# The first two products of a decoder layer: input in column quarters, both products fed together, zero products ahead of the input

## The chip, the cores and the metric

The kernel runs on one core of one Trainium2 chip. The metric is the device time of one execution in microseconds; a lower time is better. The time before is the median of three runs.

## The reference, cut to what matters

One inference step of a hybrid decoder layer, for a prompt of 512 tokens and 8 sample tokens (520 columns in all), width 1024. The normalised input is multiplied by one wide matrix, whose column groups feed three branches; the branches are gated, merged and added to the input, and a convolutional feed-forward network follows.

```python
h = rmsnorm(x, p['norm1_g'])
z = h @ p['w_in']                      # za, zq, zk, zv, zc, zg
za, zq, zk, zv, zc, zg = jnp.split(z, SPLITS, axis=-1)
...
lam = (jnp.exp(jnp.sum(p['b_lq1'].astype(f32) * p['b_lk1'].astype(f32)))
       - jnp.exp(jnp.sum(p['b_lq2'].astype(f32) * p['b_lk2'].astype(f32))) + lam_init)
o = diff_attention(q, k_all.reshape(b, -1, N_HEADS_B, 2, HEAD_DIM_B), v_all, start_pos, lam)
...
x = x + merged @ p['w_o']
f, conv_tail = conv_ffn(rmsnorm(x, p['norm2_g']), conv_prefix, p['f_up'], p['f_conv_w'], p['f_conv_b'], p['f_down'])
```

## The kernel before

All work is laid out with features on the 128 partitions and the 520 tokens as columns. The program is a list of slots (`plan`), each of which is one product: 128 columns of a weight matrix (eight blocks of 128 rows, 512 KB) by the whole activation. `zq0` to `zq3`, `zk0` to `zk3`, `zv0` to `zv3`, `z0` to `z3` and so on are slots 0, 1, 2, ... of the input projection, one for each 128 output columns.

Products keep float32 accuracy by splitting both operands into a high and a low part. A weight block `raw` becomes `wh` (a cast on ScalarE, L95) and `wl` (the difference, L96). An activation row block k becomes `Hh[k]` (`hi`, ScalarE, L450: the transposed input `xT` times the norm's gain) and `Hl[k]` (`lo`, VectorE, L453). A block (k, t) of a product is a pair of matmuls of 260 columns (L187): t = 0 is `wh` by high, t = 1 `wh` by low, t = 2 `wl` by high. So a slot is 24 pairs, 48 matmuls, in one of two PSUM accumulators (`pg`, two buffers); `evac` empties it.

`run_slot(n)` emits, in this order: the split of the weights of slot n+1, the load of those of slot n+3 (three `raw` buffers), the slot's `before` functions, then the 24 pairs with steps of the waiting chains in between. A chain is a generator: `advance` resumes the first ones of the turn after each k. A plain `yield` ends a chain's part in this slot; `yield True` puts it at the end of the turn of the same slot (`wait(4)` yields True four times). Each engine executes what was emitted for it in that order.

`begin` is written out by hand: it loads x, transposes it on TensorE into `xT` through four PSUM banks (`TP`, tag "t", handed out in rotation), and does the first product, `g_first`, interleaved with that. Its inputs come as two column halves for each 128-token tile, each followed by half of the first weights. GpSimd makes `wl` of the first product and, for k = 7, `h7` and the low part. Then it calls slot 0's `before` functions (`consts2`: constants built on GpSimd and VectorE; `chan_rows`), starts `norm1` (sums of squares on ScalarE, `ss` cleared on VectorE first) and evacuates the first product on ScalarE. `norm1` keeps reading the untransposed x.

`lam_rows` starts in slot 1: it issues five small loads, and after one yield computes lambda on VectorE and ScalarE (L332 to L338) and spreads it over the partitions by a matmul, `t_lam` (L341). `dec_softmax` (L818) transposes the scores `S_all` of cached keys into three banks (`s_dec`, `t_nk`); `pool` (L924) does a 128x512 product `s_c` (L946) for each of four groups; `attn` takes two banks for scores (`s_a`), later one for transposes (`t_a`) and one for outputs (`o_a`).

Of the kernel before, what the change touches and what calls it, by code (L numbers as in the profile page):

```python
# [45 lines left out]
class Layer:  # L46
# [276 lines left out]
    def lam_rows(self):  # L323
        nc, i = self.nc, self.i
        q = nc.sync
        self.ptab = self.C("ptab", [1, NB * NPG], I32)
        q.dma_start(self.ptab, i["page_table"].rearrange("(o a) b -> o (a b)", o=1))
        lr = self.T("lr", n=256)[0:1].rearrange("p (a d) -> p a d", a=4)
        for n, nm in enumerate(("b_lq1", "b_lq2", "b_lk1", "b_lk2")):
            q.dma_start(lr[:, n, :], i[nm])  # L330
        yield
        nc.vector.tensor_scalar(out=self.ptab, in0=self.ptab, scalar1=0, scalar2=N_POOL - 1, op0=ALU.max, op1=ALU.min)  # L332
        ls = self.C("ls", [1, 4])
        nc.vector.tensor_tensor(out=lr[:, 0:2], in0=lr[:, 0:2], in1=lr[:, 2:4], op=ALU.mult)
# [83 lines left out]

    def begin(self):
        nc, i = self.nc, self.i  # L420
        flat = lambda t: t.rearrange("p a b -> p (a b)")
        xr = [flat(self.B(f"x{t}"))[:, 0:D] for t in range(NT)] + [flat(self.B("xs"))[0:NB, 0:D]]
        nr = self.T("n1r", n=P)[0:KD]
        nc.scalar.dma_start(nr, i["norm1_g"][0].rearrange("(k p) -> k p", p=P))
        nc.scalar.dma_start(xr[NT], i["x_sample"].rearrange("b o d -> (b o) d"))
        for a in range(2):
            c = slice(a * 512, (a + 1) * 512)
            for t in range(NT):
                nc.sync.dma_start(xr[t][:, c], i["x_prompt"][0, t * P:(t + 1) * P, c])
            self.w_load(0, a)  # L430
        self.w_load(1)
        self.w_load(2)
        self.consts()
        n1 = self.C("n1", [P, KD])
        xT = [self.B("xT0"), self.B("xT1")]
        H = self.hp.tile([P, KD, NTOK], F32R, tag="Hh", name="Hh"), self.hp.tile([P, KD, NTOK], F32R, tag="Hl", name="Hl")
        self.hx = [(H[0][:, k], H[1][:, k]) for k in range(KD)]

        def turn(t, a, act):
            n = P if t < NT else NB  # L440
            tp = self.TP(f"t_x{t}{a}")
            for k in range(4):
                c = (4 * a + k) * P
                nc.tensor.transpose(tp[:, k * n:(k + 1) * n], xr[t][:, c:c + P], self.ident[0:n, 0:n])
            (nc.scalar.copy if act else nc.vector.tensor_copy)(
                xT[a][:, :, t * P:t * P + n], tp[:, 0:4 * n].rearrange("p (k t) -> p k t", k=4)
            )
# [7 lines left out]
        raw = self.raw.pop(0)  # L455
        wh, wl = (self.ws.tile([P, KD, P], F32R, tag=f"w{x}", name=f"w{x}_first") for x in "hl")
        wsp = lambda c: self.split(wh[:, c:c + 4], wl[:, c:c + 4], raw[:, c:c + 4], pool=True)
        ps = self.G("g_first")
        mm = lambda k, t: self.mm(ps, wh, wl, self.hx, k, t, k == t == 0, k == KD - 1 and t == 1)
        for t in range(NT):  # L460
            turn(t, 0, t == 1)
            if t == 1:
                tp = self.TP("t_n1")
                nc.tensor.transpose(tp[:, 0:KD], nr, self.ident[0:KD, 0:KD])
                nc.vector.tensor_copy(n1, tp[:, 0:KD])
                turn(NT, 0, 0)
        wsp(0)
        hi(0)
        turn(0, 1, 0)
        mm(0, 0)  # L470
        lo(0)
        hi(1)
        turn(1, 1, 0)
        turn(NT, 1, 0)
        hi(2)
        turn(2, 1, 0)
        mm(1, 0)
        turn(3, 1, 0)
        mm(2, 0)
        hi(3)  # L480
        mm(3, 0)
        wsp(4)
        for k in range(4, KD):
            hi(k)
        h7 = self.T("h7", n=NTOK)
        nc.gpsimd.tensor_scalar(out=h7, in0=xT[1][:, 3], scalar1=n1[:, 7:8], scalar2=None, op0=ALU.mult)
        nc.gpsimd.tensor_tensor(out=H[1][:, 7], in0=h7, in1=H[0][:, 7], op=ALU.subtract)
        for k in range(1, 7):
            lo(k)
        self.w_split(1)  # L490
        self.w_load(3)
        for k in range(4):
            mm(k, 2)
        for k in range(4):
            mm(k, 1), mm(k + 4, 0)
        for t in (2, 1):
            for k in range(4, KD):
                mm(k, t)
        self.slots[0][5]()
        self.start(self.norm1(xr, xT))  # L500
        self.slots[0][4](ps[:, :, 0:HALF])

    def norm1(self, xr, xT):
        nc = self.nc
# [313 lines left out]
    def dec_softmax(self, b0, b1):  # L818
        nc = self.nc
        n = 8 * (b1 - b0)  # L820
        m = n // 2
        if b0 == 0:
            self.wdz = self.B("wdz").rearrange("p a b -> p (a b)")
            nc.gpsimd.memset(self.wdz, 0.0)
            self.wn = self.C("wn", [NB, NH])
        pt = self.K(f"dp{b0}").rearrange("p a b -> p (a b)")[0:n]
        sp = [self.TP(f"s_dec{a}") for a in range(2)]
        for g in range(NPG):
# [21 lines left out]
        for g in range(NPG):  # L850
# [11 lines left out]
            out=wn, in_=wp[0:NB, 256:256 + m].rearrange("p (b h) -> p h b", h=NH), op=ALU.add, axis=AX.X  # L862
# [61 lines left out]
    def pool(self, j, win, zp, zs):  # L924
        nc = self.nc
# [3 lines left out]
        for l in range(j + 1):  # L929
            sh, lo = 1 << l, (2 << l) - 1  # L930
# [21 lines left out]
        ps = self.TP("s_cs")  # L952
        for g in range(4):
# [3 lines left out]
            out=ocs, in0=ps[:, 0:32].rearrange("p (j b) -> p j b", j=4),  # L957
            in1=self.cols[:, 8:12].unsqueeze(2).to_broadcast([P, 4, NB]), op=ALU.mult,
# [393 lines left out]
    def run(self):  # L1352
        self.plan()
        with self.tc.manual_schedule():
            self.begin()
            for n in range(1, len(self.slots)):
                self.cur = self.slots[n][0]
                self.run_slot(n)
            while self.chains:
                self.turn = list(self.chains)  # L1360
                self.advance()
                while self.micro:
                    self.small(1)
# [34 lines left out]
```

## Time and profile before

| | |
|---|---|
| median of 3 runs | 903.24 us (902.83 to 903.92) |
| the profiled execution | 902.99 us, of which the span from first to last instruction 901.0 us |
| TensorE busy in the span | 881.0 us (98%) |
| VectorE, ScalarE, GpSimd busy | 578.0, 340.1, 25.3 us |
| mean granted TensorE clock | 0.993 of full speed |
| 0 to 100 us: TensorE, VectorE, ScalarE busy | 90.94, 61.12, 47.24 us |
| 200 to 300 us: TensorE, VectorE, ScalarE busy | 97.18, 90.69, 49.35 us |

Times in the views count from the span's start. A busy TensorE is not TensorE at its peak: matmuls overlap, and at half clock one takes about twice as long. The idle time in front of an instruction is put down to what released it.

### The profile page before, as it was taken

How to read it: one execution, taken by the hardware profiler on the slowest of the kernel's cores; microseconds unless marked ns; L12 is line 12 of the kernel's file. 1: busy time of each engine (PE TensorE's matmuls, PEld its weight loads, DVE VectorE, ACT ScalarE, POOL GpSimd, SP SyncE). 2: the span in 40 equal slices, each digit the busy share in tenths (PEclk: the TensorE clock that was granted, in tenths of full speed). 3: DMA queues.
4: the chain of work that ended last, by engine and by line, in shares of the span. 5: the costliest groups of instructions: out<-in, count | busy, mean ns of one | idle time of the engine just before them, and what ended most of it. 6: DMA issues, size and time to landing. Idle time of an engine off the chain costs nothing.

```text
span 901.0 us, 17445 instructions
## 1 busy us (share of the span) xinstructions
PE 881.0 (98%) x7151; PEld 843.7 (94%) x7151; DVE 578.0 (64%) x970; ACT 340.1 (38%) x537; POOL 25.3 (3%) x80
## 2 busy tenths in 40 slices
PE   7899999999999999999999999999999999999998
PEld 6899987898998989889989999999999999999998
DVE  5367899879899533425775577775347777774332
ACT  4455433437532412212334334443124444442122
POOL 4000000000000000000000000000000000000000
PEclk9899999999999999999999999999999999999999
DMA  6636663426675566753443323323333333333242
GB/s 189 219 111 201 202 199 96 152 86 204 216 232 158 165 194 215 237 162 93 147 130 94 94 82 106 88 84 91 91 95 94 95 94 95 94 92 91 80 113 60
DMA packets 170467, 120.31 MB, mean 134 GB/s; under 512 B 6232, under 2 KB 149909, under 8 KB 169860
## 3 DMA queue, kind: packets, MB, share of 16 engines
q1 hardware_dynamic: 170157, 118.47, 43.5%
q8 instruction: 56, 0.92, 0.4%
q10 hardware_dynamic: 231, 0.73, 0.3%
q14 instruction: 23, 0.19, 0.1%
HBM read 112.45 MB, written 7.14 MB: 133 GB/s over the span
## 4 chain that ended last, share of the span: by engine, by line
PE 86%; DVE 9%; ACT 2%; issue 1%; DMA 1%; SPq 0%; ACTq 0%; DVEq 0%
PE g_f L187 28%; PE g_d L187 13%; PE g_ag L187 5%; PE g_bg L187 5%; PE g_o L187 5%; PE g_cg L187 3%; PE g_ap L187 3%; PE g_zk L187 3%; PE g_u L187 3%; PE g_va L187 3%; PE g_z L187 2%; PE g_zq L187 2%; PE o_dec L786 2%; PE g_zv L187 1%; DVE S_all L745 1%
## 5 line engine op out<-in xcount | busy, mean ns | idle before, releaser
L187 PE MATMUL g_f<-H2h,wl_f 128*128 128x260 f32 x704 | 141.9, 283 | 0.0
L187 PE MATMUL g_f<-H2h,wh_f 128*128 128x260 f32 x704 | 141.8, 282 | 0.0
L187 PE MATMUL g_f<-H2l,wh_f 128*128 128x260 f32 x704 | 141.7, 283 | 0.0
L187 PEld LDWEIGHTS g_f<-H2h,wh_f 128*128 128x128 f32 x704 | 108.5, 188 | 0.0
L187 PEld LDWEIGHTS g_f<-H2h,wl_f 128*128 128x128 f32 x704 | 108.5, 188 | 0.0
L187 PEld LDWEIGHTS g_f<-H2l,wh_f 128*128 128x128 f32 x704 | 108.2, 188 | 0.0
L187 PE MATMUL g_d<-ah,wh_d 128*128 128x260 f32 x340 | 69.2, 285 | 0.0
L187 PE MATMUL g_d<-al,wh_d 128*128 128x260 f32 x340 | 68.4, 283 | 0.0
L187 PE MATMUL g_d<-ah,wl_d 128*128 128x260 f32 x340 | 68.3, 282 | 0.0
L92 DVE SCALAR_TENSOR_TENSOR cv<-up,cv,cv 128x511 f32<-128x511 f32 x88 | 65.6, 746 | 2.9 <-ACT cv L1157 1.3
L95 ACT CAST wh_f<-wr_f 128x1024 fp32r<-128x1024 f32 x44 | 46.1, 1048 | 52.7 <-PE g_f L187 32.7
L1184 DVE TENSOR_TENSOR yT<-g_d,yT 128x520 f32<-128x520 f32 x23 | 16.1, 700 | 71.3 <-PE g_d L187 71.2
L1143 DVE TENSOR_TENSOR up<-g_f,rB 128x520 f32<-128x520 f32 x44 | 30.8, 700 | 47.3 <-PE g_f L187 45.3
L96 DVE TENSOR_TENSOR wl_f<-wr_f,wh_f 128x1024 fp32r<-128x1024 f32 x44 | 54.5, 1238 | 5.7 <-ACT wh_f L95 1.5
L187 PEld LDWEIGHTS g_d<-ah,wl_d 128*128 128x128 f32 x340 | 52.4, 188 | 0.0
L187 PEld LDWEIGHTS g_d<-ah,wh_d 128*128 128x128 f32 x340 | 52.2, 188 | 0.1
L187 PEld LDWEIGHTS g_d<-al,wh_d 128*128 128x128 f32 x340 | 52.2, 188 | 0.0
L95 ACT CAST wh_d<-wr_d 128x1024 fp32r<-128x1024 f32 (+1 forms) x24 | 23.5, 980 | 74.2 <-PE g_d L187 66.5
L760 DVE TENSOR_TENSOR kc<-kc,qB 128x1024 f32<-128x1024 f32 x32 | 38.6, 1214 | 0.0
L745 DVE TENSOR_REDUCE S_all<-kc 128x16 f32<-128x1024 f32 x32 | 38.4, 1209 | 0.0
L95 ACT CAST ah<-cv 128x520 fp32r<-128x520 f32 x22 | 13.8, 627 | 62.6 <-DVE cv L1172 62.6
L1157 ACT ACTIVATE cv<-up,cv 128x512 f32<-128x512 f32 x44 | 35.9, 816 | 0.8 <-DVE up L1143 0.8
(437 smaller groups left out, 2008.3 us busy)
## 6 DMA issues: line engine op xcount, KB each, us to landing
wr_f<-in_f_up SPq DMA_DIRECT2D x44, 512.0 KB
kc<-in_cache_k SPq DMA_DIRECT2D x64, 256.0 KB
vc<-in_cache_v SPq DMA_DIRECT2D x64, 256.0 KB
wr_d<-in_f_down SPq DMA_DIRECT2D x16, 512.0 KB
wr_cg<-in_w_in SPq DMA_DIRECT2D x8, 512.0 KB
wr_ag<-in_w_in SPq DMA_DIRECT2D x8, 512.0 KB
wr_bg<-in_w_in SPq DMA_DIRECT2D x8, 512.0 KB
wr_o<-in_w_o SPq DMA_DIRECT2D x8, 512.0 KB
```

What stands on the lines that cost most here:

```text
L92: self.nc.vector.scalar_tensor_tensor(out=out, in0=in0, scalar=s, in1=in1, op0=op0, op1=op1)
L95: self.nc.scalar.copy(hi, src)
L96: (self.nc.gpsimd if pool else self.nc.vector).tensor_tensor(out=lo, in0=src, in1=hi, op=ALU.subtract)
L187: self.nc.tensor.matmul(ps[:, a, 0:HALF], wt, xt[:, a * HALF:(a + 1) * HALF], start=start, stop=stop)
L745: nc.vector.tensor_reduce(out=self.S_all[:, 2 * u:2 * u + 2, b, :], in_=kt.rearrange("p (g c d) -> p g c d", g=2, d=64), op=ALU.add, axis= ...
L760: nc.vector.tensor_tensor(out=k3, in0=k3, in1=qB[b].unsqueeze(1).to_broadcast([P, 2, 512]), op=ALU.mult)
L786: nc.tensor.matmul(acc[q:q + 32], self.wdz[:, c:c + 32], vt[:, j * 512:(j + 1) * 512], start=(page < 4), stop=(page >= NB * NPG - 4), tile ...
L1143: nc.vector.tensor_tensor(out=split2(u), in0=pv, in1=split2(self.rB2), op=ALU.mult)
L1157: nc.scalar.activation(c[:, 0:SEQ], u[:, 0:SEQ], AF.Identity, bias=self.cb[:, m:m + 1], scale=self.cw2[:, m:m + 1])
L1184: nc.vector.tensor_tensor(out=split2(xj), in0=pv, in1=split2(xj), op=ALU.add)
```

## The change

- The input arrives as four quarters of 256 columns, each in two loads of 256 tokens; between them come the halves of the weights of the first two products.
- `begin` does both first products, interleaved block by block in a written order, and `run` starts with slot 2. Their split weights lie in tiles of pool `K`; both `wl` are made on VectorE, and `h7` is gone: `lo(7)` runs on VectorE as the others.
- `turn(a, q, act)` transposes two token tiles by two column blocks into one bank and copies the bank out by one instruction. The sample tokens and the gain are transposed together in `rest`.
- `keep(n)` emits n matmuls of a zeroed bf16 tile into a bank that nobody reads: 24 ahead of the first transposes, 6 ahead of the first product.
- At the end of `begin`, the split of slot 2, two weight loads and the first step of `norm1` are emitted, then both evacuations, then the `before` functions of slots 0 and 1.
- `lam_rows` yields once more before its VectorE work and once more before `t_lam`. `dec_softmax` and `pool` pass four steps before their matmuls.

```diff
@@ lam_rows
         yield
+        yield
         nc.vector.tensor_scalar(out=self.ptab, in0=self.ptab, scalar1=0, scalar2=N_POOL - 1, op0=ALU.max, op1=ALU.min)
...
         self.nlam = self.C("nlam", [P, 1])
+        yield
         t = self.TP("t_lam")
@@ begin
+        idle = self.C("idle", [P, P], BF16)
+        nc.vector.memset(idle, 0.0)
...
-        for a in range(2):
-            c = slice(a * 512, (a + 1) * 512)
-            for t in range(NT):
-                nc.sync.dma_start(xr[t][:, c], i["x_prompt"][0, t * P:(t + 1) * P, c])
-            self.w_load(0, a)
-        self.w_load(1)
+        def x_load(q):
+            c = slice(q * 256, (q + 1) * 256)
+            for a in range(2):
+                rows = i["x_prompt"][0, a * 256:(a + 1) * 256, c]
+                nc.sync.dma_start(xr[a][:, :, c], rows.rearrange("(t p) c -> p t c", p=P))
+
+        x_load(0)
+        self.w_load(0, 0)
+        x_load(1)
+        self.w_load(1, 0)
+        x_load(2)
+        self.w_load(0, 1)
+        x_load(3)
+        self.w_load(1, 1)
         self.w_load(2)
...
+        junk = self.TP("t_idle")
+
+        def keep(n):
+            for _ in range(n):
+                nc.tensor.matmul(junk[:, 0:P], idle, idle, start=True, stop=True)
+
+        def turn(a, q, act):
+            tp = self.TP(f"t_x{a}{q}")
+            for t in range(2):
+                for k in range(2):
+                    c = (2 * q + k) * P
+                    nc.tensor.transpose(tp[:, (2 * t + k) * P:(2 * t + k + 1) * P], xr[a][:, t, c:c + P], self.ident)
+            b = 2 * (q % 2)
             (nc.scalar.copy if act else nc.vector.tensor_copy)(
+                xT[q // 2][:, b:b + 2, a * 256:(a + 1) * 256].rearrange("p k (t c) -> p k t c", t=2),
+                tp.rearrange("p (t k c) -> p k t c", t=2, k=2),
             )
...
+        def wh(n, a):
+            nc.scalar.copy(w2[n][0][:, 4 * a:4 * a + 4], raw[n][:, 4 * a:4 * a + 4])
+
+        def wl(n, a):
+            c = slice(4 * a, 4 * a + 4)
+            nc.vector.tensor_tensor(out=w2[n][1][:, c], in0=raw[n][:, c], in1=w2[n][0][:, c], op=ALU.subtract)
...
+        keep(24)
+        turn(0, 0, False)
+        rest()
+        turn(1, 0, True)
         hi(0)
+        wh(0, 0)
+        keep(6)
+        mm(0, (0, 0))
         lo(0)
+        wl(0, 0)
         hi(1)
+        mm(0, (0, 1), (1, 0))
+        turn(0, 1, False)
+        mm(0, (0, 2), (1, 2))
+        lo(1)
+        turn(1, 1, True)
+        mm(0, (1, 1))
+        wh(1, 0)
+        mm(1, (0, 0), (0, 1), (1, 0), (1, 1))
+        wl(1, 0)
         hi(2)
+        mm(0, (2, 0), (2, 2))
+        mm(1, (0, 2), (1, 2), (2, 0), (2, 2))
+        lo(2)
         hi(3)
+        turn(0, 2, False)
+        mm(0, (3, 0), (3, 2), (2, 1))
+        mm(1, (3, 0), (3, 2), (2, 1))
+        lo(3)
+        turn(1, 2, True)
+        wh(0, 1)
+        hi(4)
+        mm(0, (3, 1), (4, 0))
+        mm(1, (3, 1))
+        lo(4)
+        wl(0, 1)
+        turn(0, 3, True)
+        hi(5)
+        mm(0, (4, 1), (5, 0), (4, 2), (5, 2))
+        lo(5)
+        turn(1, 3, False)
+        wh(1, 1)
+        mm(1, (4, 0), (4, 1), (5, 0))
+        mm(0, (5, 1))
+        mm(1, (5, 1))
+        wl(1, 1)
+        hi(6)
+        mm(0, (6, 0), (6, 2))
+        mm(1, (4, 2), (5, 2), (6, 0), (6, 2))
+        lo(6)
+        hi(7)
+        mm(0, (7, 0), (7, 2), (6, 1))
+        lo(7)
+        mm(0, (7, 1))
+        mm(1, (7, 0), (7, 2), (6, 1), (7, 1))
+        self.w_split(2)
         self.w_load(3)
+        self.w_load(4)
+        xt = [xr[t // 2][:, t % 2] for t in range(NT)] + [xs]
+        norm = self.norm1(xt, xT)
+        next(norm)
+        for n in range(2):
+            self.slots[n][4](ps[n][:, :, 0:HALF])
+        for n in range(2):
+            self.slots[n][5]()
+        self.start(norm)
@@ dec_softmax
+        yield from self.wait(4)
         pt = self.K(f"dp{b0}").rearrange("p a b -> p (a b)")[0:n]
@@ pool
         yield
+        yield from self.wait(4)
         ps = self.TP(f"s_c{j}")
@@ run
-            for n in range(1, len(self.slots)):
+            for n in range(2, len(self.slots)):
```

## Rows read from the trace of the kernel before

**Rows 1.** Waits of TensorE, whole span: us in total, times, longest.
```profile
PE t_lam L341 <- DVE ls L338: 3.9, 1, 3.9
PE s_c L946 <- ACT p L649: 2.0, 1, 2.0
PE s_dec L829 <- DVE S_all L745: 1.8, 2, 1.1
```

**Rows 2.** Chain that ended last, 0 to 60 us: start, length, what.
```profile
21.90 5.95 PE g_zq L187 x48
...
34.89 11.51 PE g_zq L187 x78
46.40 1.44 PE g_zk L187 x12
```

**Rows 3.** The same chain, 100 to 400 us.
```profile
117.09 5.78 PE g_z L187 x48
```

**Rows 4.** Timeline of VectorE, 20 to 34.5 us; brackets: idle before, releaser.
```profile
24.58 0.16 DVE L273 TENSOR_SCALAR lab<-pi 128x1 int32<-128x1 int32 x1 [2.26 <-POOL pi L270]
...
27.76 0.06 DVE L507 MEMSET ss<- 128x5 f32 x1
31.52 1.23 DVE L96 TENSOR_TENSOR wl_zq<-wr_zq,wh_zq 128x1024 fp32r<-128x1024 f32 x1 [3.69 <-ACT wh_zq L95]
```

**Rows 5.** Timeline of ScalarE, 20 to 34.5 us.
```profile
27.87 1.06 ACT L511 ACTIVATE j<-x 128x1024 f32<-128x1024 f32 x1 [4.40 <-DVE ss L507]
...
29.97 0.57 ACT L533 COPY zq<-g_zq 128x520 f32<-128x520 f32 x1
```

**Rows 6.** TensorE by stretches: us, busy (count), granted clock, DMA share, GB/s.
```profile
35.00:39.00 4.00, 4.00 (x19) 0.50 1.01 311
...
138.70:140.60 1.90, 0.00 (x1) 1.00 0.45 156
141.60:144.60 3.00, 3.00 (x15) 0.50 0.00 0
```

**Rows 7.** Groups, 0 to 22 us: busy us, mean ns | idle before.
```profile
L445 DVE COPY xT<-t_x 128x512 f32<-128x512 f32 x7 | 4.8, 692 | 8.3 <-PE t_x L444 8.3
...
L96 DVE TENSOR_TENSOR wl_zq<-wr_zq,wh_zq 128x1024 fp32r<-128x1024 f32 x1 | 1.3, 1304 | 0.0
...
L95 ACT CAST wh_first<-wr_zq 128x512 fp32r<-128x512 f32 x2 | 1.2, 617 | 0.9 <-DMA wr_zq<-in_w_in 0.9
...
L445 ACT COPY xT<-t_x 128x512 f32<-128x512 f32 x1 | 0.6, 586 | 3.1 <-PE t_x L444 3.1
```

**Rows 8.** Timeline of all engines, 0 to 32 us.
```profile
3.60 1.08 PE L444 MATMUL t_x<-ident,x 128*128 128x128 f32 x4 [3.60 <-DMA x<-in_x_prompt]
...
5.04 1.11 PE L444 MATMUL t_x<-ident,x 128*128 128x128 f32 x4 [0.35 <-DMA x<-in_x_prompt]
...
9.51 2.58 ACT L450 ACTIVATE Hh<-xT,n 128x520 fp32r<-128x520 f32 x4 [1.24 <-DVE xT L445]
...
10.92 0.75 DVE L92 SCALAR_TENSOR_TENSOR Hl<-xT,n,Hh 128x520 fp32r<-128x520 f32 x1
...
13.74 1.05 PE L444 MATMUL t_x<-ident,x 128*128 128x128 f32 x4
```

**Rows 9.** Timeline of TensorE, 131 to 133 us.
```profile
132.59 0.40 PE L643 MATMUL s_a<-maskb,identb 128*128 128x128 bf16 x4
```

**Rows 10.** Groups of TensorE instructions, 8 to 14 us.
```profile
L187 PE MATMUL g_first<-Hh,wh_first 128*128 128x260 f32 x4 | 1.6, 498 | 0.0
```

**Rows 11.** Groups of TensorE instructions, 24 to 28 us.
```profile
L187 PE MATMUL g_zq<-Hl,wh_zq 128*128 128x260 f32 x12 | 2.6, 282 | 0.0
```

**Rows 12.** Timeline of all engines, 209 to 247 us.
```profile
222.45 0.40 PE L829 MATMUL s_dec<-ident,S_all 128*40 128x128 f32 x2 [1.06 <-DVE S_all L745]
```

**Rows 13.** Timeline of all engines, 126 to 147 us.
```profile
136.49 1.50 PE L676 MATMUL o_a<-vtok,wT 128*128 128x128 f32 x12
...
140.66 1.20 PE L946 MATMUL s_c<-pl,mixc 128*128 128x512 f32 x2 [1.96 <-ACT p L649]
```

More of the change, by code (lines that the diff above doesn't have):

```diff
@@ L420, in begin @@
         nc, i = self.nc, self.i
-        flat = lambda t: t.rearrange("p a b -> p (a b)")
-        xr = [flat(self.B(f"x{t}"))[:, 0:D] for t in range(NT)] + [flat(self.B("xs"))[0:NB, 0:D]]
+        idle = self.C("idle", [P, P], BF16)
+        nc.vector.memset(idle, 0.0)
+        xr = [self.B(f"x{a}").rearrange("p a b -> p (a b)")[:, 0:2 * D].rearrange("p (t d) -> p t d", t=2) for a in range(2)]
+        xs = self.B("xs").rearrange("p a b -> p (a b)")[0:NB, 0:D]
         nr = self.T("n1r", n=P)[0:KD]
         nc.scalar.dma_start(nr, i["norm1_g"][0].rearrange("(k p) -> k p", p=P))
-        nc.scalar.dma_start(xr[NT], i["x_sample"].rearrange("b o d -> (b o) d"))
-        for a in range(2):
-            c = slice(a * 512, (a + 1) * 512)
-            for t in range(NT):
-                nc.sync.dma_start(xr[t][:, c], i["x_prompt"][0, t * P:(t + 1) * P, c])
-            self.w_load(0, a)
-        self.w_load(1)
+        nc.scalar.dma_start(xs, i["x_sample"].rearrange("b o d -> (b o) d"))
+        def x_load(q):
[11 more added lines that the diff above has]
+        self.w_load(1, 1)
         self.w_load(2)
@@ L437, in begin, with rest @@
         self.hx = [(H[0][:, k], H[1][:, k]) for k in range(KD)]
[L439 to L444, printed above, removed]
+        junk = self.TP("t_idle")
[9 more added lines that the diff above has]
+            b = 2 * (q % 2)
             (nc.scalar.copy if act else nc.vector.tensor_copy)(
-                xT[a][:, :, t * P:t * P + n], tp[:, 0:4 * n].rearrange("p (k t) -> p k t", k=4)
-            )
+                xT[q // 2][:, b:b + 2, a * 256:(a + 1) * 256].rearrange("p k (t c) -> p k t c", t=2),
+                tp.rearrange("p (t k c) -> p k t c", t=2, k=2),
+            )
+        def rest():
+            tp = self.TP("t_n1")
+            nc.tensor.transpose(tp[:, 0:KD], nr, self.ident[0:KD, 0:KD])
+            for k in range(KD):
+                nc.tensor.transpose(tp[:, KD * (k + 1):KD * (k + 2)], xs[:, k * P:(k + 1) * P], self.ident[0:NB, 0:NB])
+            nc.vector.tensor_copy(n1, tp[:, 0:KD])
+            for a in range(2):
+                c = KD + 32 * a
+                nc.vector.tensor_copy(xT[a][:, :, SEQ:NTOK], tp[:, c:c + 32].rearrange("p (k t) -> p k t", k=4))
         def hi(k):
@@ L453, in lo @@
             self.stt(H[1][:, k], xT[k // 4][:, k % 4], n1[:, k:k + 1], H[0][:, k], ALU.mult, ALU.subtract)
[L455 to L466, printed above, removed]
@@ L467, in begin @@
-        wsp(0)
+        raw = [self.raw.pop(n) for n in range(2)]
+        w2 = [[self.K(f"wf{n}{x}", F32R).rearrange("p a b -> p (a b)")[:, 0:KD * P].rearrange("p (k c) -> p k c", c=P)
+               for x in "hl"] for n in range(2)]
+        ps = [self.G(f"g_first{n}") for n in range(2)]
+        done = set()
+        def wh(n, a):
[3 more added lines that the diff above has]
+            nc.vector.tensor_tensor(out=w2[n][1][:, c], in0=raw[n][:, c], in1=w2[n][0][:, c], op=ALU.subtract)
@@ L468, in begin, with mm @@
+        def mm(n, *kt):
+            for k, t in kt:
+                first = not any(d[0] == n for d in done)
+                done.add((n, k, t))
+                last = sum(d[0] == n for d in done) == 3 * KD
+                self.mm(ps[n], *w2[n], self.hx, k, t, first, last)
+        keep(24)
+        turn(0, 0, False)
+        rest()
+        turn(1, 0, True)
         hi(0)
-        turn(0, 1, 0)
-        mm(0, 0)
+        wh(0, 0)
+        keep(6)
+        mm(0, (0, 0))
         lo(0)
+        wl(0, 0)
@@ L472, in begin @@
         hi(1)
-        turn(1, 1, 0)
-        turn(NT, 1, 0)
+        mm(0, (0, 1), (1, 0))
[7 more added lines that the diff above has]
+        wl(1, 0)
         hi(2)
[L476 to L479, printed above, removed]
+        mm(0, (2, 0), (2, 2))
+        mm(1, (0, 2), (1, 2), (2, 0), (2, 2))
+        lo(2)
         hi(3)
-        mm(3, 0)
@@ L482, in begin @@
[L482 to L490, printed above, removed]
-        self.w_load(3)
[L492 to L501, printed above, removed]
+        turn(0, 2, False)
[11 more added lines that the diff above has]
+        hi(5)
@@ new lines, in begin @@
+        mm(0, (4, 1), (5, 0), (4, 2), (5, 2))
[15 more added lines that the diff above has]
+        mm(1, (7, 0), (7, 2), (6, 1), (7, 1))
+        assert len(done) == 6 * KD
+        self.w_split(2)
```

## Prediction

> **What bounds the kernel now.** I read the waits of TensorE first. Three are worth naming: 3.9 us before `t_lam`, 2.0 us before `s_c`, 1.8 us in two parts before `s_dec` [rows 1]. Everywhere else products follow each other without a gap, so a change gains only what it takes from these waits, from the start, or from time at half clock.
>
> Next the chain that ended last, over the first 60 us, for the marks to measure against. The second product's 48 matmuls run from 21.90 to 27.85, and `zk0`, the fifth product, begins at 46.40 [rows 2]. Between lie `zq2` and `zq3`, 96 matmuls. Forty-eight undisturbed ones take 5.78 us, 0.120 each [rows 3], so these need 11.5 us plus about 0.2 of transposes; they have 18.55.
>
> The timelines of VectorE and ScalarE say why. `consts2` is emitted after the first product; its first VectorE instruction waits 2.26 us for GpSimd, which comes late because it had split weights and made `h7`. The memset of `ss` follows at 27.76 [rows 4]. ScalarE waits 4.40 us for it, does two squares, and only at 29.97 empties the second product and then makes the next `wh` [rows 5]. VectorE's `wl` starts at 31.52, having waited 3.69 us [rows 4], and the lambda work sits behind that, so TensorE, in order, stands at `t_lam`.
>
> Last the clock. After that stand it is granted 0.50 in 35 to 39; after the 1.9 us stand before `s_c` it falls as well, to 0.50 in 141.6 to 144.6 [rows 6]. The 78 matmuls behind `t_lam` take 11.51 us [rows 2] where 0.120 each makes 9.4: 2.1 lost.
>
> **Lambda later.** The added yields put its VectorE work into slot 4 and `t_lam` into slot 5, a product after its operand; `nlam` is first read in slot `z0`. The 3.9 us wait goes with its 2.1 us of half clock. With `begin` emptying GpSimd of splits and `h7`, the constants are ready long before `consts2` needs them on VectorE, so nothing takes the wait's place behind slot 2. Both are worked into the mark at `zk0` below. Cover for the lambda work there: VectorE and ScalarE have only one split and one evacuation in a 5.8 us slot. If that cover were gone, at most 3.9 us returns.
>
> **The new `begin`, walked through in its written order.** Prices: evacuation 0.69 on VectorE, 0.59 on ScalarE; a half of `wh` 0.62; `wl` of a whole tile 1.30, so 0.65 the half, now on VectorE instead of GpSimd [rows 7]; `hi` 0.65 (four in 2.58); `lo` 0.75 [rows 8]. A pair of matmuls is 0.24, four transposes about 0.46 at full clock.
> Input: the first two 256 KB of x let TensorE start at 3.60 and 5.04 [rows 8]; the same sizes now. The last piece of x was in by 13.74 [rows 8]; 256 KB more go ahead of it, under 1 us, and its transposes come only at 18.4 and 20.9 below. So arrival sets the start alone. Issuing 8 x loads as before, in another form, with the weights between, is hidden with it.
> The 24 zero products begin near 1 us. The nearest row is the mask's bf16 products, four in 0.40 [rows 9]: 0.06 apart at full clock, I take 0.12 at half: 2.9 us, done at 4.0. Bounds: 0.06 ends at 2.5 and costs nothing; 0.22, the spacing of the fp32 transposes, ends at 6.4 and delays the first product 2.4 us.
> Then at full clock: second transposes to 5.6, ScalarE copy 6.2, `hi0` 6.9, `wh` 7.5, first product 7.55; `hi1` 8.15, transposes, VectorE copy 9.7, `lo1` 10.45; `wh` of the second weights 11.15. From 11.2 TensorE has 16 pairs and eight transposes without a hole: 16.0. Copy 16.6, `wh` 17.2, `hi4` 17.85; a pair waits for it 1.7 us. Transposes 18.85, copy 19.5, `hi5` 20.2 (a wait of 1.2). Last transposes 21.4, copy 22.2, `hi7` 23.5. TensorE's last 14 pairs run from 22.9 to 26.3, against 27.85 before.
> But the second evacuation order undoes that. `begin` emits the split of slot 2 and two squares of `norm1` ahead of both evacuations on ScalarE: `wh` 24.5, VectorE's `wl` 25.8, memset, squares 2.2 (as [rows 5] have them) 28.1, evacuation 28.7; some 0.3 for handovers, 29.0. Both product buffers are taken, so `zq2` can't start before 29.0; TensorE stands 2.4 to 2.7 us. This is what becomes late next.
>
> **The clock in `begin`.** The profile's granted column reads 1.00 there, but a product at 8 to 14 us took 498 ns [rows 10], where the same shape takes 282 later [rows 11]: TensorE ran at the lower level although it had transposed and multiplied since 3.6. With zero products ahead of the input I expect full speed earlier, but not throughout, since the walk above leaves TensorE gaps between 7 and 11 us. I take half clock up to about 11: 1.2 us on the chain, `zq2` at 30.2. Bounds: 29.0 at full clock from the first product; 32.0 at half clock until 15, as before.
> The Trainium skill (TensorE: Matmul & The Clock Gate, Part 1) says that "the default state is throttled, and activity releases the throttle". By it alone the zero products would release it before the first real one, and the start would be the 29.0 of the first rival; the 498 ns behind ten microseconds of such activity speak against taking it whole.
>
> **Sum to `zk0`.** 30.2 + 11.5 + 0.2 = 41.9 against 46.40: 4.5 earlier. The stand of 2.4 to 2.7 us lies between the two after which the clock fell, 1.9 and 3.9, so I let it fall: half of the nearer case's 3 to 3.9 us, 1.7 lost (0 if it holds, 2.1 by the other). Left: 2.8.
>
> **`dec_softmax` later.** Its eight transposes stood behind the last `S_all` reduction, 1.06 us at 222.45 [rows 12] and 0.7 later. Four steps are 2.9 us of product, so the reduction is through. VectorE is nearly full there, so part returns as waits for `wl`: 1.0 of 1.8 (0.3 to 1.8).
>
> **`pool` later.** `s_c` waited 1.96 us because the bank it takes in rotation still held `s_a`, whose exponentials came late. Moving it doesn't free the bank: counting the four banks in emission order, the third after `s_a` now goes to the second `o_a` of that slot (two `o_a` ran at 136.49 [rows 13]), a product step earlier. The moved `s_c` also takes 0.66 us of VectorE out of the way. 0 taken; bounds 0.4 lost to 3.5 gained (1.96 and half of 3 us at half clock).
>
> **Total.** 2.8 + 1.0 + 0 = 3.8. The profiled execution took 902.99 with a span of 901.0, 0.25 under the median, so 899.4 against the median 903.24. Differences under 0.2%, 1.8 us, can't be told from none.
>
> **Rivals.**
> First, the zero products bring the clock up for good and the stand at `zq2` doesn't lower it: 29.0 + 11.7 = 40.7, 5.7 gained, 6.7 with `dec_softmax`: 896.5. For it: TensorE is dense from 1 to 4. Against: the stand, and 498 ns.
> Second, `s_c`'s wait does go, because the exponentials arrive sooner than I count: 3.5 on top of the forecast or the first rival, 892.9 to 895.9. Against: the bank count.
> Third, the products start at half clock as before, until 15: `zq2` at 32.0, `zk0` at 43.7, 1.7 lost to the stand: 1.0 left, and 0.3 to 1.0 of `dec_softmax` less 0.4: 901 to 902.5, no change that shows. For it: sparse work from 7 to 11.
> Fourth, the other side: half clock through the whole of both products. 96 matmuls at 0.21 (19 in 4.00 us [rows 6]) are 20.2, 24 transposes at 0.22 5.3: from 7.9 to 33.4, evacuation and handover 0.9, `zk0` at 46.0, and 4 us more at half clock lose 2: 48.0, 1.6 late; with the bank's 0.4, 905. It decides once `zq2` starts after 34.7. Against: dense products lifted the clock in 35 to 39.5.
>
> **Chances.** Forecast (897.5 to 901) 0.40, first 0.20, second 0.15, third 0.17, fourth 0.08. The forecast and the first two are faster, and a quarter of the third: 0.79. The rest of the third is the same, and a little of the fourth: 0.14. Slower 0.07. Range 893.5 to 902.5: it reaches into the second and third and leaves out the deepest sum of gains and the fourth.
>
> **What will show it.** `t_lam` without a wait and `consts2` on VectorE without one for GpSimd; `zq2`'s first matmul at about 30, released by ScalarE's evacuation after two squares; granted clock 0.50 for 3 to 4 us behind it; `zk0` at about 43.5; no wait before `s_dec`; one of about 2 us at 137, before `o_a` or `t_a`. The forecast is wrong if TensorE is dense earlier than 11 us or `zq2` starts before 28, if `hi4` and `hi5` are no waits, or if x in 1 KB pieces lands late.

## The result, and the profile after

The kernel after the change takes 916.85 us in the median (916.51 to 917.04, four runs) against 903.04 (902.35 to 903.92, four runs): a ratio of 1.0152, 95% interval 1.0134 to 1.0170. It is slower by 13.8 us; the prediction was 899.4, with 0.07 for slower. The profiled execution took 917.04 us with a span of 915.3, TensorE busy for 887.7 us (97%), VectorE 577.3, ScalarE 342.1, GpSimd 17.6, the mean granted clock 0.990. The engines do the same work as before, but for the 30 zero products of TensorE. TensorE waits more, 27.6 us of the span against 20.0, and its busy time is 6.7 us longer, since more of it runs at half clock. Two later executions, one of e2 at 3004 us and one of e6 at 1719 us, lie far outside all others and are left out of the medians and ratios below.

The waits of TensorE of the kernel after (total, times, longest) answer to [rows 1]:

```profile
PE o_a L746 <- ACT p L719: 4.4, 2, 4.1
PE g_first L187 <- ACT Hh L480: 2.6, 2, 1.6
PE t_a L734 <- ACT p L719: 2.6, 1, 2.6
PE s_a L707 <- DVE ocs L1028: 2.2, 1, 2.2
PE g_zq L187 <- ACT zq L603: 1.9, 1, 1.9
PE g_ap L187 <- DVE dsm L916: 1.9, 1, 1.9
PE g_first L187 <- ACT wf0h L492: 1.3, 1, 1.3
```

The three waits of before are gone, `t_lam`, `s_c` and `s_dec`, 7.7 us in all. In their place stand seven others with 16.9 us, in three places: the input (`g_first`, `g_zq`), the pool and attention stretch (`o_a`, `t_a`, `s_a`) and the gate (`g_ap`). At the start the kernel before also waited 4.5 us for pieces of x; the kernel after waits 1.1 us there, for the tile of the zero products.

To place the loss, the first start of a product's matmuls, from the tile views of both profiles:

| | `zk0` | `z0` | `cg0` | `bg0` | `f` |
|---|---|---|---|---|---|
| before, us | 46.2 | 100.5 | 209.7 | 384.5 | 509.7 |
| after, us | 47.0 | 101.8 | 219.7 | 398.3 | 523.8 |
| lost since the mark before it | 0.8 | 0.5 | 8.7 | 3.8 | 0.3 |

The sum, 14.1, is the difference of the two profiled executions. `pool` lies between `z0` and `cg0`, both parts of `dec_softmax` (`s_dec` at 238.4 and 304.9) between `cg0` and `bg0`.

**The start.** The chain of the kernel after from `zq2` on (start, length), against [rows 2]:

```profile
33.55 8.30 PE g_zq L187 x54
42.01 5.20 PE g_zq L187 x42
47.21 2.16 PE g_zk L187 x18
```

And the timeline of all engines that leads to it:

```profile
9.16 0.80 PE L187 MATMUL g_first<-Hh,wf0h 128*128 128x260 f32 x2 [1.30 <-ACT wf0h L492]
...
21.40 0.51 PE L187 MATMUL g_first<-Hh,wf0h 128*128 128x260 f32 x2 [1.57 <-ACT Hh L480]
...
23.89 0.80 PE L187 MATMUL g_first<-Hh,wf0h 128*128 128x260 f32 x2 [1.06 <-ACT Hh L480]
...
30.83 1.06 ACT L581 ACTIVATE j<-x 128x1024 f32<-128x1024 f32 x1 [1.31 <-DVE ss L577]
...
32.93 1.06 ACT L603 COPY zq<-g_first 128x520 f32<-128x520 f32 x2
...
33.55 0.56 PE L187 MATMUL g_zq<-Hh,wh_zq 128*128 128x260 f32 x2 [1.93 <-ACT zq L603]
```

Read the lengths of the pairs: the same two matmuls take 0.80 at 9.16 and at 23.89, 0.51 at 21.40. The engine runs at half speed in `begin` twice: from the start until about 13 us, and again behind 23.89. The last three lines are a stand (TensorE idle in front of an instruction) that the prediction's walk through `begin` had found: two squares of `norm1` ahead of the evacuations, and `zq2` behind those.

**The pool stretch.** The timeline of VectorE and TensorE of the kernel after, 130 to 197 us, against [rows 13]:

```profile
136.94 0.69 DVE L92 SCALAR_TENSOR_TENSOR pl<-ws,zp 128x509 f32<-128x509 f32 x1 [0.93 <-PE s_c L1018]
...
142.38 1.02 PE L746 MATMUL o_a<-vtok,wT 128*128 128x128 f32 x6 [4.09 <-ACT p L719]
...
152.39 0.69 DVE L92 SCALAR_TENSOR_TENSOR pl<-ws,zp 128x505 f32<-128x505 f32 x1 [4.41 <-PE s_c L1018]
...
158.01 0.55 PE L734 MATMUL t_a<-ident,p 128*128 128x128 f32 x3 [2.63 <-ACT p L719]
...
196.20 0.89 PE L707 MATMUL s_a<-kT,qT 64*128 64x128 f32 x6 [2.15 <-DVE ocs L1028]
```

Two kinds of wait are to be seen. `o_a` reads `vtok` and `wT`, and yet waits for the exponentials `p`; `s_a` reads `kT` and `qT`, and yet waits for `ocs`. Neither reads what it waits for, so each waits for a bank: `p` is the last reader of the bank of `s_a`, `ocs` of that of `s_cs`. And VectorE waits for `s_c` before it writes `pl`: the tile `pl` is one of nine that go round, and the one it gets still has to be read by the late product `s_c`. What stands behind `pl` on VectorE, the maxima of the scores, comes late by that, and so do the exponentials that `t_a` needs.

The granted clock of the kernel after, by stretches as in [rows 6] (the number behind the five engines' columns), fell after such stands:

```profile
23.00:27.00 4.00, 3.11 (x14) 3.11 (x15) 1.32 (x2) 1.34 (x3) 0.00 (x0) 0.58 0.45 131
...
34.00:37.00 3.00, 3.00 (x16) 3.00 (x16) 1.23 (x1) 3.00 (x5) 0.00 (x0) 0.50 0.10 24
...
198.00:201.00 3.00, 3.00 (x16) 3.00 (x15) 2.64 (x8) 1.66 (x8) 0.00 (x0) 0.50 0.06 16
```

### The profile page after: what moved, and what is told of

Read it like the earlier page. It is cut to its first block, busy times and chain, and to the rows that moved or that the text cites. A ratio compares the mean times of both kernels' runs of the same rounds, so it can differ in the third digit from the quotient of the medians.

```text
span 915.3 us, 17519 instructions
## 1 busy us (share of the span) xinstructions
PE 887.7 (97%) x7181; PEld 849.9 (93%) x7181; DVE 577.3 (63%) x972; ACT 342.1 (37%) x541; POOL 17.6 (2%) x76
## 4 chain that ended last, share of the span: by engine, by line
PE 88%; DVE 7%; ACT 3%; issue 1%; DMA 0%; POOL 0%; SPq 0%; DVEq 0%; ACTq 0%; POOLq 0%
PE g_f L187 28%; PE g_d L187 13%; PE g_bg L187 5%; PE g_o L187 5%; PE g_ag L187 5%; PE g_cg L187 5%; PE g_ap L187 3%; PE g_zk L187 3%; PE g_z L187 2%; PE g_va L187 2%; PE g_cp L187 2%; PE o_dec L856 2%; PE g_zq L187 1%; PE g_zv L187 1%; PE g_u L187 1%
## 5 line engine op out<-in xcount | busy, mean ns | idle before, releaser
L95 ACT CAST ah<-cv 128x520 fp32r<-128x520 f32 x22 | 13.8, 627 | 62.7 <-DVE cv L1244 62.7
```

Of the source, the lines that this page charges most:

```text
L95: self.nc.scalar.copy(hi, src)
```

## The experiments

The theory after the trace: the two chains' four steps of waiting cost most of the 13.8 us, above all the one in `pool`; the new `begin` gives back all that the later lambda wins. Rival: the new `begin` makes everything behind it late, and the waits further on only show it. In what follows "us" beside a kernel is the median of its timed runs, with the ratio to the kernel before run on the same chip; stages are differences of the marks used above, of one profiled execution each. Differences between experiments mix chips, on which the kernel before took 902.35 to 904.0 us; by the ratios they come out up to 1 us higher or lower.

**e1: the change without the two waits.**

```diff
@@ dec_softmax, pool
-        yield from self.wait(4)
```

> The changed kernel without the four steps in pool and without those in dec_softmax; begin and the lambda yields stay. Theory: the loss behind the first projection comes from these two moves alone (pool: the first products of va to those of cg start 9.5 us later relative to before; dec_softmax about 4), while begin with the lambda yields is about 1 us slower up to z0. So about 904.5 us, with the waits of before at s_c (2 us) and s_dec (1.8 us) back and none at o_a of 4 us. Rival: the later losses come from the other timing that begin hands on; then 912 or more and the 4 us wait stays.

903.82 us, ratio 1.0008 (0.9998 to 1.0018): all that was lost is back. `z0` to `cg0` is 109.1 us (after 117.9, before 109.2), `cg0` to `bg0` 174.5 (178.6, 174.8). `zk0` stays at 46.9: what is left of the change, `begin` and lambda, is worth nothing.

**e2 and e3: one of the two waits each.** e2 keeps that of `dec_softmax`, e3 that of `pool`.

> The changed kernel with pool as before; the four steps in dec_softmax stay. Theory: pool's move is the larger part, so 907 to 909 us: the 904.5 of the kernel without both, plus 3 to 4 for dec_softmax. Rival, by which moving dec_softmax gains the 1.8 us that it waited: 903.

> The changed kernel with dec_softmax as before; the four steps in pool stay. Theory: 912 to 914 us, since pool's move alone puts the 4 us wait before o_a and the 2.6 us wait before t_a there. Rival (dec_softmax is the larger part): 908 or less.

e2: 905.75 us, 1.0025 (1.0008 to 1.0042). e3: 911.14, 1.0104 (1.0074 to 1.0133). So `pool` is the larger: `z0` to `cg0` is 117.2 in e3 and 109.0 in e2. Over e1 the two make 1.9 and 7.3, in sum 9.2 of the 13.0 between e1 and after. By stages 12.9 us are found (8.8 and 4.1 us longer in after than in e1). In e3's profile `begin` was by chance 3.1 us quicker than in after, `zk0` at 43.9.

**e4: the kernel before with lambda later, and nothing else.**

```diff
@@ lam_rows
         yield
+        yield
...
+        yield
         t = self.TP("t_lam")
```

> The kernel before with only the two yields in lam_rows. Theory: the 3.9 us wait at t_lam and the 2.1 us lost at half clock behind it go and nothing takes their place: 897 us (6 gained). Rival: VectorE and ScalarE are late there anyway because of consts2 and the squares, and the wait passes to the next product's weights: 900 to 903, with a wait before g_zq on wl or zq.

896.95 us, 0.9926 (0.9904 to 0.9948). Two lines of the change are worth 6.1 us against the 903.04 (5.4 against the 902.35 of the same chip, 4.7 to 8.7 by the interval). `zk0` starts at 38.7 against 46.2. The new `begin` therefore costs 6.9 us: e1, which has it, against e4, which has not.

**e5: evacuations ahead of `norm1`'s first step, on e1.**

```diff
@@ begin
-        norm = self.norm1(xt, xT)
-        next(norm)
         for n in range(2):
             self.slots[n][4](ps[n][:, :, 0:HALF])
+        norm = self.norm1(xt, xT)
+        next(norm)
```

> The changed kernel without the moves in pool and dec_softmax, and with the two evacuations at the end of begin ahead of norm1's first squares. Theory: the stand of 1.9 us before zq2 comes from ScalarE's two squares; without it zq2 starts about 31.5 instead of 33.5 and the clock doesn't fall behind it: 899.5 to 901 against 903.8. Rival: the squares only move into the next product and delay its weights; 903 to 904, with a wait on wl later.

902.18 us, 0.998 (0.9961 to 0.9998): 1.6 us better than e1, at the edge of what can be told. The stand before `zq2` is gone, which starts at 32.0 with the clock held.

**e6 and e8: the zero products ahead of the input.** e6 takes all 30 from e1; e8 adds 24 to e4.

> The changed kernel without the moves in pool and dec_softmax and without any zero product (24 and 6 left out). Theory: the zero products bring the clock up only in some executions and for a short while, so leaving them out changes the time by under 1 us either way; first transposes start at 3.6 instead of 4.0: 903 to 905. Rival, by which they hold the clock up: 906 or more.

> The kernel before with the two yields in lam_rows and 24 zero products ahead of the first transposes. Theory: the first product is paced by input and by the other engines, so the clock there is worth little: 896 to 898, as without them (897.0). Rival, by which the half clock until 15 us costs: 894 or less.

e6: 904.2 us, 1.0012 (1.0000 to 1.0025), against e1's 1.0008. e8: 897.1, 0.9933 (0.9908 to 0.9957), against e4's 0.9926. By the times, neither tells them from nothing. Single profiles differ: the first pair took 0.80 us in e4 and 0.50 in e8, where the 24 zero products stood ahead:

```profile
10.04 0.80 PE L187 MATMUL g_first<-Hh,wh_first 128*128 128x260 f32 x2
```

```profile
10.27 0.50 PE L187 MATMUL g_first<-Hh,wh_first 128*128 128x260 f32 x2 [0.76 <-ACT Hh L454]
```

But behind the zero products of the new `begin` it took 0.80 in the kernel after, e1, e2, e3 and e5, and 0.52 in e7.

**e9: zero products in the stands of `begin`, on e5.** Two groups of blocks are taken apart for it, and each group of zero products takes a bank of its own.

```diff
-        keep(6)
+        keep(14)
...
+        keep(8)
         mm(1, (0, 0), (0, 1), (1, 0), (1, 1))
...
-        mm(0, (3, 1), (4, 0))
-        mm(1, (3, 1))
+        mm(0, (3, 1))
+        mm(1, (3, 1))
+        keep(24)
+        mm(0, (4, 0))
...
-        mm(0, (4, 1), (5, 0), (4, 2), (5, 2))
+        mm(0, (4, 1), (4, 2))
+        keep(16)
+        mm(0, (5, 0), (5, 2))
...
         hi(6)
+        keep(12)
         mm(0, (6, 0), (6, 2))
```

> Kernel e5_evacuate_first (both chains without their waits, evacuations ahead of the first step of norm1) with zero products also in the stands of begin: 14 ahead of the first product, then 24, 16 and 12 ahead of the blocks that wait for the high parts 4, 5 and 6, and 8 ahead of the second product's first block. Theory, half clock in begin is what the new begin pays: with the stands filled, the pairs run at 0.24 us from about 9 us on, zk0 starts at 40 to 41.5 against 43.8, and the time is 899 to 900. Rival, the order sets the pace, each engine's waits for the next copy, high part and split: zk0 stays at 43 to 44 or comes later by the zero products that stand in the way, 902 to 903.

899.3 us, 0.9948 (0.9931 to 0.9966), 2.9 less than e5, as the theory had it (the intervals just touch); `zk0` at 40.8 (e5 43.8). The two profiles by the same stretches, first e5, then e9:

```profile
12.00:16.00 4.00, 3.34 (x15) 3.04 (x15) 1.39 (x2) 2.35 (x4) 0.00 (x0) 0.50 0.65 160
16.00:20.00 4.00, 4.00 (x31) 4.00 (x30) 1.36 (x2) 0.00 (x0) 0.00 (x0) 0.82 0.00 0
20.00:24.00 4.00, 1.77 (x13) 1.36 (x12) 1.36 (x2) 2.58 (x5) 0.00 (x0) 1.00 0.00 0
24.00:28.00 4.00, 3.59 (x17) 3.59 (x18) 1.79 (x3) 1.11 (x3) 0.00 (x0) 0.57 0.45 131
```

```profile
12.00:16.00 4.00, 3.66 (x34) 3.43 (x34) 1.39 (x2) 2.35 (x4) 0.00 (x0) 1.00 0.69 174
16.00:20.00 4.00, 4.00 (x47) 3.79 (x45) 1.37 (x3) 1.73 (x3) 0.00 (x0) 1.00 0.00 0
20.00:24.00 4.00, 3.91 (x39) 3.56 (x39) 2.27 (x4) 1.72 (x3) 0.00 (x0) 1.00 0.34 98
24.00:28.00 4.00, 4.00 (x42) 3.96 (x41) 3.60 (x5) 2.30 (x3) 0.00 (x0) 1.00 0.51 148
```

In e5 TensorE idles for 2.2 of the four us from 20 to 24, and the clock is 0.57 in the next four. In e9 zero products fill the stands, the clock stays at 1.00 from 12 on. Still e9 reaches `zk0` 2.1 us after e4. Of the 6.9 us of the new `begin`, the evacuation order makes 1.6 (e5) and e9's step 2.9; 2.3 are left, which no run takes apart further. The 2.9 are put down to the clock, though the two groups that changed place came with it.

**e10 and e11: the two waits on e4's `begin`.**

> Kernel e4_before_lambda_later (the kernel before with the two yields in lam_rows alone) with the four steps of waiting in dec_softmax. Theory, ScalarE's order: the wait before s_dec goes, but the second exponential, with the two table loads around it, stands in front of the gate's sigmoid and the casts behind it, so the stretch from cg0 to bg0 grows by about 2.5 us: 899 to 900 against 897. Rival, as predicted: 1.8 us of waiting goes and 0.8 comes back, 896.

> Kernel e4_before_lambda_later with the four steps of waiting in pool. Theory, the loss lies in pool's own rotation of tiles and banks and not in what begin left behind: z0 to cg0 grows from about 108 to 116 us, 904 to 905. Rival, it takes the new begin, whose norm1 and lambda work come later, to make the banks late: 897 to 899.

e10: 899.11 us, 0.9945 (0.9928 to 0.9962), 2.2 over e4, with intervals that overlap. The timeline of ScalarE, VectorE and TensorE, first of e4, 285 to 288 us, then of e10, 286 to 303 us, shows what became of the 1.8 us:

```profile
285.27 1.21 DVE L842 TENSOR_REDUCE dmx<-dp 24x1 f32<-24x1032 f32 x1
...
286.74 1.28 ACT L845 ACT_TABLE_LOAD   x1 [2.32 <-DVE dmx L843]
```

```profile
289.38 0.70 DVE L1044 TENSOR_TENSOR sgc<-g_cg,rB 128x520 f32<-128x520 f32 x1 [5.40 <-PE g_cg L187]
...
290.22 1.22 DVE L96 TENSOR_TENSOR wl_ag<-wr_ag,wh_ag 128x1024 fp32r<-128x1024 f32 x1
291.36 1.21 DVE L843 TENSOR_REDUCE dmx<-dp 24x1 f32<-24x1032 f32 x1
292.61 0.14 DVE L844 TENSOR_SCALAR dmx<-dmx 24x1 f32<-24x1 f32 x1
292.82 1.28 ACT L846 ACT_TABLE_LOAD   x1 [2.64 <-DVE dmx L844]
...
295.37 1.28 ACT L1049 ACT_TABLE_LOAD   x1
296.67 0.64 ACT L1049 ACTIVATE sgc<-sgc 128x520 f32<-128x520 f32 x1
297.34 0.70 DVE L1060 TENSOR_TENSOR mg<-g_cp,sgc 128x520 f32<-128x520 f32 x1 [4.59 <-ACT sgc L1049]
297.72 1.92 ACT L95 CAST oah<-u 128x2080 fp32r<-128x2080 f32 x1
...
299.68 2.33 DVE L96 TENSOR_TENSOR oal<-u,oah 128x2080 fp32r<-128x2080 f32 x1 [1.04 <-ACT oah L95]
...
302.06 0.51 PE L187 MATMUL g_ap<-oal,wh_ap 128*128 128x260 f32 x2 [1.85 <-DVE dsm L848]
```

The exponential of the decode scores stands, with two table loads around it, in front of the gate's sigmoid and of the cast `oah`. It did so in e4 too; but it now starts 3.9 us later, counted from `cg0` (201.4 in e4, 203.6 in e10): the scores leave their banks later, and the maximum that it needs (`dmx`) has come behind `sgc` and `wl_ag` on VectorE, of which `sgc` waits 5.40 us for its product. So the cast `oah` and the difference `oal` end late; TensorE waits 0.56 us for the one and 1.85 for the other, whose end at 302.01 is the one that counts at `g_ap`, though the view names `dsm`. The stretch from `cg0` to `bg0` is a weak witness here: 177.2 us in e10, 176.8 in e4, 174.8 in e8, where nothing in it was changed. The rest of the 2.6 us between the two profiles lies ahead of it (0.9 before `zk0`, 1.2 from `z0` to `cg0`), where e10 changed nothing.

e11: 906.59 us, 1.0037 (1.0026 to 1.0049), 9.6 over e4, and `z0` to `cg0` 118.8 against 108.0: there TensorE idles 10.3 us against 3.2, and its busy time is 3.7 longer, at a granted clock of 0.96 against 1.00. The loss needs nothing of the new `begin`; the rival has fallen.

**e12: one step instead of four in `dec_softmax`, on e8.**

> Kernel e8_zero_products_alone (the kernel before, lambda later, 24 zero products ahead) with one step of waiting in dec_softmax instead of four. Theory: one step is 0.72 us of product, less than the 1.06 and 0.7 us of waiting before s_dec, so these shrink to a few tenths, and the exponential moves by less than a step: cg0 to bg0 shorter by 0.5 to 1.5, 895.5 to 896.5 against 897.1. Rival: any step puts the exponential in front of the sigmoid, 898 or more.

897.01 us, 0.993 (0.9913 to 0.9946), no different from e8. The waits before `s_dec` are gone, but 1.9 us before `g_cp` (for `mg`) and 1.2 before `g_cg` (for `sgc`) have come, and `cg0` to `bg0` is 178.2 us in its profile against 174.8: the number of neither theory, and no gain.

**e7, e13 to e16: tiles or banks in `pool`?** e7 (on e3) and e14 (on e11) give `pl` two buffers of its own; e13 names the bank of `s_c` ahead of the four steps; e15 also writes eight columns into it there, and e16 has both.

```diff
@@ pool (e7, e14, e16)
-        pl = self.T(f"pl{j}", n=SEQ)
+        pl = self.cv3[:, (j % 2) * SEQ:(j % 2 + 1) * SEQ]
@@ pool (e15, e16; e13 without the matmul)
-        yield from self.wait(4)
         ps = self.TP(f"s_c{j}")
+        nc.tensor.matmul(ps[:, 0:8], self.ident, self.ident[:, 0:8], start=True, stop=True)
+        yield from self.wait(4)
```

> The changed kernel without the move in dec_softmax, with that in pool, but with pl in two buffers of its own instead of the nine tiles that rotate. Two theories for pool's loss of 7.3 us. Tiles: VectorE waits up to 4.4 us for s_c before it may write the next pl, and so makes the scores' maxima late; then this kernel loses that wait and the 2.6 us wait at t_a, and takes 905 to 907. Banks alone: the wait before o_a and the others stay; 910 to 912. I expect the first with the wait at o_a left at about 3 us.

> Kernel e11_pool_wait_alone (lambda later and the four steps of waiting in pool) with the bank of s_c taken ahead of the four steps instead of behind them, so that the banks go round in the order of the kernel before, while the product s_c itself stays late. Theory, the loss of e11 (906.6 against 897.0) is half order of banks and half the tile pl that VectorE waits for: the 4.1 us before o_a and the 2.2 before s_a go, VectorE's 4 to 5 us before pl stay with the 2.6 before t_a, z0 to cg0 falls from 118 to about 112, and the time is 900 to 902. Rival one, tiles alone: 905 to 907. Rival two, banks alone: 897 or less.

> Kernel e11_pool_wait_alone (lambda later and the four steps of waiting in pool) with pl in two buffers of its own, halves of one tile that the constants of the convolution share later. Theory, the tile that VectorE waits for is a third of the loss (as in e7) and the banks the rest: VectorE's wait before pl goes, the 2.6 before t_a goes, of the 4.1 before o_a about 3 stay, and the 2.2 before s_a stays; 904 to 906 against 906.6. Rival, the tile is the whole loss: 897 to 899.

> Kernel e11_pool_wait_alone with a product of 8 columns written into the bank of s_c ahead of the four steps, so that the bank is taken at that place, as in the kernel before, while the product s_c stays late (in e13 the bank was only named ahead of the steps, and the instructions came out the same). Theory, the order of the banks is half of the loss: the 4.1 before o_a and the 2.2 before s_a go, 2.0 come back before the small product, VectorE's wait before pl and what it delays stay; 901 to 904. Rival, tiles and the moved work are the loss and the banks only where it shows: 906 to 908.

> Kernel e15_bank_taken_early with pl in two buffers of its own. Theory, banks and tiles together were the whole loss: all waits of TensorE in pool but the 2.0 of the kernel before are gone, and the time is that of e4_before_lambda_later, 896 to 898.5. Rival, a third cause: the moved evacuations cost VectorE and ScalarE their place in line, 900 or above.

| | us | ratio | `z0` to `cg0` |
|---|---|---|---|
| e3 | 911.14 | 1.0104 (1.0074 to 1.0133) | 117.2 |
| e7, its own tiles | 910.19 | 1.0083 (1.0058 to 1.0108) | 114.2 |
| e11 | 906.59 | 1.0037 (1.0026 to 1.0049) | 118.8 |
| e13, bank named early | 906.84 | 1.0049 (1.0033 to 1.0065) | 117.6 |
| e14, own tiles | 902.23 | 0.9991 (0.9981 to 1.0001) | 114.1 |
| e15, bank written early | 913.2 | 1.0116 (1.0089 to 1.0143) | 125.0 |
| e16, both | 904.4 | 1.0014 (1.0001 to 1.0027) | 115.2 |

The timeline of e11, then that of e14, then that of e15, 130 to 155 us:

```profile
134.90 1.65 PE L678 MATMUL o_a<-vtok,wT 128*128 128x128 f32 x6 [4.10 <-ACT p L651]
...
145.69 0.68 DVE L92 SCALAR_TENSOR_TENSOR pl<-ws,zp 128x505 f32<-128x505 f32 x1 [5.19 <-PE s_c L949]
...
151.30 0.55 PE L666 MATMUL t_a<-ident,p 128*128 128x128 f32 x3 [2.62 <-ACT p L651]
```

```profile
134.14 1.05 PE L679 MATMUL o_a<-vtok,wT 128*128 128x128 f32 x6 [2.93 <-ACT p L652]
```

```profile
135.32 1.65 PE L678 MATMUL o_a<-vtok,wT 128*128 128x128 f32 x6 [4.10 <-ACT p L651]
...
148.40 0.69 DVE L92 SCALAR_TENSOR_TENSOR pl<-ws,zp 128x505 f32<-128x505 f32 x1 [7.48 <-PE s_c L950]
...
154.01 0.39 PE L947 MATMUL s_c<-ident 128*128 128x8 f32 x2 [3.35 <-ACT p L651]
```

With tiles of its own, VectorE waits for no `s_c`, the stand before `t_a` is gone, that before `o_a` is 1.2 us shorter, and 4.4 of the 9.6 us are back. On the new kernel (e7 against e3) the profile shows 3.0, the times only 1.0 with intervals that overlap. e13 tells nothing: the bank goes to the first instruction that writes it and not to the line that names it, so its instructions stand in e11's order. e15 goes against its forecast: the waits before `o_a` and `s_a` stay as long as before, and a wait of 3.35 us for the small product comes on top; 6.6 us worse, with own tiles (e16) 2.2. It doesn't test the order of the banks alone, though: taken early, the bank is also held through the four steps, and `o_a` still gets one whose reader is `p`. What the order is worth without the longer hold, no run shows. Of the loss 5.2 us remain in e14. By its profile TensorE idles 3.3 us longer than in e4 between `z0` and `cg0` (2.9 before `o_a` and 2.1 before `s_a` have come, both for a bank whose reader comes late, and the 2.0 before `s_c` are gone), and its busy time is 2.8 longer, at a granted clock of 0.97 against 1.00. Whether the late evacuations themselves or the work moved beside them make these readers late, no run here separates.

## Why the prediction was wrong

Of the 17.5 us between the forecast and the measured time, by the marks some 8.7 lie in the stretch of `pool`, 4.8 in that of `dec_softmax` and 3.6 ahead of `zk0`.

**The step that failed: `pool` later, "0 taken; bounds 0.4 lost to 3.5 gained".** It cost 9.6 us alone (e11 over e4; 7.3 and 11.1 in the pairs e3 over e1 and after over e2) and lengthened its stretch by 8.8 in the kernel after. I had traced the bank of the moved product and forecast that the second `o_a` would wait in its place; it did, 4.1 us and not 2. Nor did I trace the bank of `s_cs`, for which `s_a` waits 2.2 us. Above all I didn't trace the moved product's operand. `pl` is taken from tiles that go round; as long as `s_c` hasn't read it, VectorE can't write the next, and all that is queued behind that on VectorE waits too: 4.4 of the 9.6 us (e14). The view was there: a step that reads a shared tile later returns it later. The bound on the losing side, 0.4, left room for none of these waits, nor for the half clock behind them. The rest of the 9.6 stands in the traces as waits for banks and as half clock; what makes those banks late stays open.

**`begin` and lambda, 2.8 forecast, -0.8 measured.** Lambda was right: 3.9 us of stand and 2.1 of half clock were forecast, 6.1 (5.4 on the same chip) is what it is worth alone (e4). The new `begin` took all of that back. The failing term is "I take half clock up to about 11: 1.2 us". The walk had found TensorE's own gaps, at 7 to 11 us and for `hi4` and `hi5`; it charged 1.2 us of half clock for the first and none behind the others. The half clock lasted until about 13, and came back for some 3 us behind `hi5`. No engine waited for late input there: ScalarE's copies waited for TensorE's transposes (4.2, 3.7 and 3.8 us), of which the first three groups of four took 1.05 to 1.11 us where the walk had 0.46. The first product came at 9.16 instead of 7.55, the second at 14.59 instead of 11.2, the block of `hi4` at 21.40 instead of 17.85, and the last pair ended at 31.6 instead of 26.3. The stand before `zq2` was right in its cause (two squares, then the evacuations) and at 1.93 us near the 2.4 to 2.7; that the clock falls behind it was right as well: 33.55 to 47.21 is 13.7 us where 11.7 had been enough, 2.0 lost and 1.7 forecast. So the mark came near the 48.0 of the fourth rival, though not by half clock throughout: half clock until about 13 is nearer to the third rival's 15, and the dip behind `hi5` is in neither. That e9 starts `zq2` at 28.92, close to the 29.0 at full clock, is chance: it has no stand there, and its products end 2.8 us later than the walk had them.

By the sentence of the Trainium skill (TensorE: Matmul & The Clock Gate, Part 1) that the prediction weighed, activity releases the throttle. Behind the zero products and the transposes the first pair took 0.80 in the kernel after, as at half speed, and 0.50 in e8; no time shows the zero products ahead of the input, taken away or added (e6, e8). In the stands they kept the granted clock at 1.00 (e9). The traces agree with the rule where they fill gaps; where they only stand ahead, the profile of e8 agrees, that of e7 for one pair (0.52, then 0.72), and those of the kernel after, e1, e2, e3 and e5 do not.

**`dec_softmax` later, 1.0 gained.** The waits before `s_dec` went, as said. The cover failed: I named `wl` on a nearly full VectorE as what would give 0.8 back. What came late was the exponential: its maximum stood behind `sgc` and `wl_ag` on VectorE, and the sigmoid and the cast stood behind it and its two table loads on ScalarE. The cost is about 2 us in two pairs of runs (e10 over e4, e2 over e1), each time at the edge of what the intervals separate, and 5.7 beside `pool`'s step (after over e3, of which e3's quicker start may be up to 3.1); a gain of 1.0 is not to be seen in any.

**Hits on the list of what would show it.** `consts2` waited for no GpSimd, `t_lam` for nothing, `s_dec` for nothing, the second `o_a` waited at 138. None of these decided the time. The second rival, that `s_c`'s wait goes and nothing takes its place, was wrong in every kernel with the step.

## What to carry to other kernels

A step that is moved later keeps everything it will read: trace the round of its operands' buffers as well as that of its result's, and ask which in-order engine has to write the next one. A wait that is removed should be weighed with the other engines' lines: what the later step hands to them comes behind other work there, and holds up what stands behind it. When a change bundles parts, the cheapest of them can hold all the gain: e4, two lines on the kernel before, at 897 us beats both kernels, and e8 and e12 are no better.

## What the runs showed of the hardware

The same `begin`, instruction for instruction, went through different clock phases from execution to execution: `zk0` at 46.9 in e1, 47.6 in e2, 43.9 in e3. A mark from one profile of a start with gaps is good to some 4 us.

The same stand can be followed by half clock in one execution and not in another. The 2.0 us before `s_c` were followed by 0.50 in the kernel before [rows 6] and by 0.55 in e10, but by 1.00 in e4:

```profile
134.60:137.60 3.00, 3.00 (x24) 2.32 (x23) 2.85 (x9) 2.81 (x11) 0.00 (x0) 1.00 0.00 0
```

From `z0` to `cg0` the kernel before and e10 take 109.2 us, e4 108.0. And e4 has the granted clock at 0.66 between 295 and 300 us, with TensorE busy for all of the ten us ahead, where e8, with the same work there, has 1.00; from `cg0` to `bg0` e4 takes 2.0 us longer. Differences of that size between two profiles say nothing of an edit.

The granted clock read 1.00 in the kernel after from 8 to 12 us, while its pairs of 260 columns took 0.80 and 0.64 instead of 0.40. For the start, the duration of a known shape was the better witness.
